# Three pairs of column groups of a projection, half of their k tiles by Strassen's scheme

## The chip, the cores and the metric

One core of a Trainium2 chip runs the whole program. The metric is the device time of one execution in microseconds (us), as the median of several runs. The core has five engines with a queue each: TensorE (PE, matrix products; PEld is its weight load), VectorE (DVE), ScalarE (ACT), GpSimd (POOL) and SyncE (SP, which here issues nearly all DMA transfers). An engine works through its queue in order.

## The reference, cut to what matters

One decoder layer for 256 tokens, D_MODEL 2048, all in f32:

```python
h = rmsnorm(x, norm_mix_g)
u = h @ w_in                     # 2048 x 12288
c_g, b_g, xa, za, q, fl, iv, og, ga, gb = split(u)      # ga, gb: 2048 columns each
ya = b_g * causal_dwconv3(c_g * xa, conv_w) * silu(za)
yb = (gated linear recurrence of q, fl, iv, normed) * silu(og)
m = sigmoid(ga) * (ya @ w_a_out) + sigmoid(gb) * (yb @ w_b_out)
x = x + m @ w_o
x = x + sigmoid(rmsnorm(x) @ w_ple_gate) * (p @ w_ple_proj)
return rmsnorm(x, final_norm_g)
```

The change touches `ga = h @ w_in[:, ...]` and `gb`, and nothing of what is computed from them.

## The kernel before, in words

Tokens lie in two tiles (t = 0, 1) of 128. A weight matrix is cut into column groups of 512 (index j) and chunks of 256 rows (index c), so a chunk of a group is two k tiles of 128 x 512, side by side in a row of 1024. One chunk is a step of the list `steps`; the list is walked in one loop over `pos`, in an order fixed by `groups`: PP (4 groups), the 24 groups of w_in with ga and gb of j last, each pair followed by A of j (w_a, 4 chunks) and B of j (w_b, 4 chunks), then O and PG. A group of w_in has 8 chunks.

Every f32 product is made of three matmuls in a rounded format (fp32r). `split` (L115) makes the high part `whi` of a chunk on ScalarE (L129) and the low part `wlo` on VectorE (L130); the activations are kept as high and low parts too (`hT` = `xh`, `xl`). `product` (L975, matmul L980) then adds high x high, high x low and low x high into a PSUM bank. So a step is 2 k tiles x 2 token tiles x 3 = 12 matmuls of 512 columns. Splits are issued three steps ahead (`LEAD`); `whi` and `wlo` have four buffers each, so a split can begin when PE has finished the step four before.

`load` (L96) fetches two chunks (1 MB) into a `raw` buffer, of which there are three, through SyncE's queue. PSUM has four banks with the tag g and four with s; a group takes two g banks.

When a group is finished its epilogue, a generator, is put on the list `active`; after every step `advance` takes each epilogue on by one `yield`. `ep_ga` and `ep_gb` turn the banks into sigmoid tiles `ga` and `gb` (ScalarE, L260). `ep_a` multiplies `ga` by A's banks (VectorE, L670), `ep_bb` `gb` by B's banks (L677); then GpSimd adds the two (L682; VectorE for j = 3), and `turned` transposes the sum: SyncE writes it to memory (`turn<-t`, L238), reads it back (`t<-turn`, L240), and VectorE turns 32 x 32 blocks (L244). ScalarE and VectorE then split it into `mh` and `ml` (L688, L689). A Tile scheduler fixes the final order in each engine's queue.

Of the kernel before, what the change touches and what calls it, by code (L numbers as in the profile page):

```python
# [23 lines left out]
CW = 512  # L24
# [11 lines left out]
_FIELD = {"c": 0, "b": 2, "xa": 4, "za": 6, "q": 8, "f": 10, "iv": 12, "og": 14, "ga": 16, "gb": 20}  # L36
IN_ORDER = [(n, j) for j in range(2) for n in ("f", "q", "iv", "og", "c", "xa", "za", "b")]
IN_ORDER += [(n, j) for j in range(4) for n in ("ga", "gb")]


PRM_GMIX, PRM_GPLE, PRM_GHG, PRM_LB, PRM_CONV = 0, 16, 32, 40, 48
# [5 lines left out]
def hybrid_kernel(ctx, tc, xT, x, pT, prm, gfin, masks, w_in, w_a, w_b, w_o, w_pg, w_pp, out):  # L47
    nc = tc.nc
# [27 lines left out]
    def nm(s):  # L76
        uid[0] += 1
        return f"{s}_{uid[0]}"

    def t4(tag="t4", bufs=None):  # L80
        bufs = bufs or {"tmp1": 8, "tmp2": 5, "tmp3": 5}[state["tmp"]]
        return pools[state["tmp"]].tile([P, 1024], F32, tag=tag, bufs=bufs, name=nm(tag))

    def bank(tag):
        return ps.tile([P, CW], F32, tag=tag, bufs=4, name=nm(tag))
# [4 lines left out]


    stream = []
    loaded = {}
    parts = {}

    def load(pos):  # L96
        w, g, c = stream[pos]
        if pos // 2 not in loaded:
            raw = wp.tile([P, 2, 2 * CW], F32, tag="raw", bufs=3, name=nm("raw"))
            loaded[pos // 2] = raw  # L100
            if FIRST <= pos < FIRST + 20:
                for i in range(2):
                    nc.sync.dma_start(out=raw[:, i, :], in_=w[g, :, c + i, :])
            elif pos >= FIRST:
                nc.sync.dma_start(out=raw, in_=w[g, :, c : c + 2, :])
        return loaded[pos // 2]

    def load_first(pos, queues):

        w, g, c = stream[pos]  # L110
        n = 2 * CW // len(queues)
        for i, eng in enumerate(queues):
            eng.dma_start(out=load(pos)[:, pos % 2, i * n : (i + 1) * n], in_=w[g, :, c, i * n : (i + 1) * n])

    def split(pos, c0=0, c1=2 * CW):  # L115
        w, g, c = stream[pos]
        src = load(pos)[:, pos % 2, :]

        pool, n = (pools["late"], 6) if (pos - state.get("late", len(steps))) % 10 < 6 and "late" in state else (wp, 4)
        if pos not in parts:  # L120
            parts[pos] = tuple(
                pool.tile([P, 2 * CW], F32R, tag=tag, bufs=n, name=nm(tag)) for tag in ("whi", "wlo")
            )
        hi, lo = parts[pos]
        s = slice(c0, c1)
        with ExitStack() as order:
            for i in state["before"].pop() if state.get("before") else ():
                order.enter_context(tc.issue_after(i))
            a = nc.scalar.activation(out=hi[:, s], in_=src[:, s], func=AF.Copy)  # L129
            v = nc.vector.tensor_tensor(  # L130
                out=lo[:, s], in0=src[:, s], in1=hi[:, s].bitcast(F32), op=ALU.subtract
            )
        state["splits"] = (a.ins, v.ins)

    groups = []
    groups += [("PP", j, w_pp, j, "pT") for j in range(4)]
    for n, (kind, j) in enumerate(IN_ORDER):
        groups.append((kind, j, w_in, n, "hT"))
        if kind == "gb":
            groups.append(("A", j, w_a, j, "yaT"))  # L140
            groups.append(("B", j, w_b, j, "ybT"))
    groups += [("O", j, w_o, j, "mT") for j in range(4)]
    groups += [("PG", j, w_pg, j, "x1T") for j in range(4)]
    steps = []
    active, done = [], 0
    for gi, (kind, j, w, g, op) in enumerate(groups):
        for c in range(w.shape[2]):
            stream.append((w, g, c))
            steps.append((gi, c))

    last_group = len(steps) - w_pg.shape[2]


    LEAD, AHEAD = 3, 4
    TOKENS, NORM = 10, 13
    FIRST = 6

# [20 lines left out]
    def gain(base, k):  # L178
        return prm_t[:, base + k : base + k + 1]
# [471 lines left out]
        nc.vector.tensor_tensor(out=lo, in0=ya, in1=hi.bitcast(F32), op=ALU.subtract)  # L651

    def ep_ga(j, psum):
        g = t4("ga", 2)
        sig(psum, g)
        state["ga", j] = g
        yield

    def ep_gb(j, psum):
        g = t4("gb", 2)  # L660
        sig(psum, g)
        state["gb", j] = g
        yield


    def ep_a(j, psum):
        g = state["ga", j]
# [285 lines left out]
    def step(e):  # L953

        with ExitStack() as order:
            for i in state["splits"] if done < len(steps) else ():
                order.enter_context(tc.issue_after(i))
            try:
                next(e)
            except StopIteration:  # L960
                active.remove(e)

    def advance():
        for e in list(active):
            step(e)
# [9 lines left out]
    def product(psum, op, k, t, hi, lo, first, last, which=(0, 1, 2)):  # L975

        oh, ol = (x[:, k, t * P : (t + 1) * P] for x in op)
        for n in which:
            a, b = ((oh, hi), (oh, lo), (ol, hi))[n]
            nc.tensor.matmul(psum, a, b, start=first and n == 0, stop=last and n == 2)  # L980

    psum = None
    for pos, (gi, c) in enumerate(steps[:last_group]):
        kind, j, w, g, opname = groups[gi]
        nch = w.shape[2]
        if kind == "PG" and j == 0 and c == 0:
            close_pool("m")
            open_pool("late", "left")
            state["late"] = done
        order = ExitStack()  # L990
        if 1 <= pos <= 4:

            order.enter_context(tc.issue_after(state["evicted"]))
        while done < min(pos + 1 + ahead(pos), len(steps)):
# [12 lines left out]
        order.close()  # L1007
        if 2 <= pos < 6:
            load_x(pos + 2)
        if pos == 4:  # L1010
            begin()
        if 0 <= pos - NORM < 4:
            add_squares(pos - NORM)
        if pos == NORM + 3:
            norm_of_x()
        if pos == NORM + 4:
            active.append(ep_f(0, waiting))
            step(active[-1])
            nc.sync.dma_start(out=mask_t, in_=masks)
        if c == 0:  # L1020
            psum = [bank("s" if kind == "PP" and j > 1 else "g") for _ in range(NT)]
        hi, lo = parts.pop(pos)
        for i in range(2):
            k = 2 * c + i
            for c0, c1 in EARLY[0][:2] if pos == 0 and i == 0 else ((0, CW),):
                s = slice(i * CW + c0, i * CW + c1)
                for n in (((0,), (2,), (1,)), ((0,), (1,), (2,)))[i] if pos == 0 else ((0, 1, 2),):
                    for t in range(NT):
                        product(
                            psum[t][:, c0:c1], state[opname], k, t, hi[:, s], lo[:, s], k == 0 and c0 == 0,  # L1030
                            k == 2 * nch - 1, n,
                        )


        if kind == "PG" and j == 0 and c < 2:
            advance()
        for q in range(done, min(done + AHEAD, len(steps)) if pos >= FIRST else 0):
            load(q)
        if 0 <= pos - TOKENS < 4:
            load_tokens(pos - TOKENS)  # L1040
        if kind != "PG" or j or c >= 2:
            advance()
        if kind == "O" and j == 0 and c == nch - 3:
            finish()
            third_part()
        if kind == "O" and j > 0 and c == 1:
            residual(j)
        if kind == "O" and j == 2 and c == 4:
            load_gfin()
        if kind == "PG" and c == 4:  # L1050
            load_projection(j)
            if j == 2:
                load_projection(3)
        if c == nch - 1:
            if kind == "f" and j == 0:

                waiting = psum
            if kind == "ga" and j == 0:
                finish()
                second_part()  # L1060
            if kind == "O" and j == 0:
# [104 lines left out]
```

## Time and profile before

| | |
|---|---|
| median of 3 runs | 824.15 us (824.03 to 824.48) |
| profiled execution, span | 822.8 us |
| mean granted clock of TensorE | 0.997 of full speed |
| PE busy, instructions | 813.9 us (99%), 4236 |
| VectorE busy | 531.4 us (65%) |
| ScalarE busy | 433.1 us (53%) |
| GpSimd busy | 91.1 us (11%) |
| DMA, mean | 228 GB/s |

The timed runs and the profiled one are different executions; the profile shows its own span, from the first to the last instruction, and no other time of it. Busy shares are means over the run, made of stages with different limits, so the prediction reads the stages that are changed. Matmuls are pipelined: a row's length (0.39 us) is longer than the distance to the next row.

### The profile page before, as it was taken

Reading aid. Unit: us, or ns where it says so; the run is one execution under the profiler, and the core shown is the slowest. Engines: PE = TensorE matmul, PEld = TensorE weight load, DVE = VectorE, ACT = ScalarE, POOL = GpSimd, SP = SyncE. Lnnn points to the kernel's source line nnn. Section 1 sums busy time; section 2 is a strip of 40 time slices with the busy share of each in tenths; the row PEclk is TensorE's granted clock in tenths of the full one; section 3 lists DMA queues with packets and bytes.
Section 4 is the critical chain, followed back from the end, with each engine's and each line's share of the span. In section 5 each row is a group of like instructions: output and inputs, shape, how many; then the busy total and the mean of one; then the engine's idle time right before and its main releaser. Section 6 shows DMA issues by size and latency. Waiting matters only on the chain.

```text
span 822.8 us, 10787 instructions
## 1 busy us (share of the span) xinstructions
PE 813.9 (99%) x4236; PEld 675.9 (82%) x4236; DVE 531.4 (65%) x620; ACT 433.1 (53%) x559; POOL 91.1 (11%) x75
## 2 busy tenths in 40 slices
PE   9999999999999999999999999999999999999996
PEld 7888888888888888888888888888888888888885
DVE  5746698967766598877646545545645656678734
ACT  7666565555564465466443543544444445566522
POOL 1000045300000064200001001000100000001210
PEclk9999999999999999999999999999999999999998
DMA  9969656648776665748555755766755698888702
GB/s 333 365 274 339 222 180 210 219 155 258 255 234 225 204 205 161 251 153 279 202 191 182 268 182 179 256 205 202 228 190 198 221 316 290 282 301 283 301 0 104
DMA packets 41524, 187.27 MB, mean 228 GB/s; under 512 B 4736, under 2 KB 14208, under 8 KB 24320
## 3 DMA queue, kind: packets, MB, share of 16 engines
q1 hardware_dynamic: 41328, 186.31, 66.0%
q8 instruction: 33, 0.54, 0.3%
q10 hardware_dynamic: 144, 0.26, 0.1%
q14 instruction: 19, 0.16, 0.0%
HBM read 172.92 MB, written 13.63 MB: 227 GB/s over the span
## 4 chain that ended last, share of the span: by engine, by line
PE 97%; DMA 1%; issue 1%; DVE 0%; ACT 0%; SPq 0%; ACTq 0%; POOLq 0%; POOL 0%
PE g L980 95%; DMA raw<-in_w_pp 1%; PE s L980 1%; PE s L394 1%; PE s L527 0%; PE s L551 0%; PE s L550 0%; PE s L549 0%; ACT xs L803 0%; DVE wlo L130 0%; ACT whi L129 0%; ACTq L1161 0%; POOLq L1161 0%; POOL tot L789 0%; ACT t L761 0%
## 5 line engine op out<-in xcount | busy, mean ns | idle before, releaser
L130 DVE TENSOR_TENSOR wlo<-raw,whi 128x1024 fp32r<-128x1024 f32 (+1 forms) x295 | 367.8, 1252 | 248.6 <-ACT whi L129 247.7
L129 ACT ACTIVATE whi<-raw 128x1024 fp32r<-128x1024 f32 (+1 forms) x295 | 307.8, 1050 | 327.1 <-PE g L980 293.7
L980 PE MATMUL g<-whi,xl 128*128 128x512 f32 (+1 forms) x912 | 351.4, 385 | 0.0
L980 PE MATMUL g<-wlo,xh 128*128 128x512 f32 (+1 forms) x912 | 351.4, 385 | 0.0
L980 PE MATMUL g<-whi,xh 128*128 128x512 f32 (+1 forms) x912 | 351.1, 386 | 0.0
L980 PEld LDWEIGHTS g<-whi,xl 128*128 128x128 f32 x912 | 171.3, 188 | 34.5
L980 PEld LDWEIGHTS g<-whi,xh 128*128 128x128 f32 x912 | 171.3, 188 | 34.2
L980 PEld LDWEIGHTS g<-wlo,xh 128*128 128x128 f32 x912 | 171.3, 188 | 34.1
L980 PE MATMUL g<-whi,mh 128*128 128x512 f32 x128 | 49.8, 389 | 0.0
L980 PE MATMUL g<-wlo,mh 128*128 128x512 f32 x128 | 49.8, 389 | 0.0
L980 PE MATMUL g<-whi,ml 128*128 128x512 f32 x128 | 49.6, 389 | 0.0
L682 POOL TENSOR_TENSOR t<-ga,gb 128x512 f32<-128x512 f32 x6 | 10.6, 1788 | 198.3 <-DVE gb L677 198.3
L980 PE MATMUL g<-whi,yaTh 128*128 128x512 f32 (+1 forms) x74 | 28.3, 389 | 0.1
L980 PE MATMUL g<-wlo,yaTh 128*128 128x512 f32 (+1 forms) x74 | 28.0, 385 | 0.2 <-DVE wlo L130 0.2
L980 PEld LDWEIGHTS g<-wlo,mh 128*128 128x128 f32 x128 | 24.0, 188 | 5.0
L980 PEld LDWEIGHTS g<-whi,mh 128*128 128x128 f32 x128 | 24.0, 188 | 5.0
L980 PEld LDWEIGHTS g<-whi,ml 128*128 128x128 f32 x128 | 24.0, 188 | 4.9
L448 POOL TENSOR_TENSOR t<-b 128x512 f32<-128x512 f32 x10 | 20.4, 2036 | 68.8 <-DMA t<-turn 41.0
L980 PE MATMUL g<-whi,yaTl 128*128 128x512 f32 (+1 forms) x74 | 27.9, 383 | 0.0
L980 PE MATMUL g<-whi,ybTh 128*128 128x512 f32 x64 | 24.9, 389 | 0.0
L980 PE MATMUL g<-wlo,ybTh 128*128 128x512 f32 x64 | 24.9, 389 | 0.0
L980 PE MATMUL g<-whi,ybTl 128*128 128x512 f32 x64 | 24.9, 389 | 0.0
(160 smaller groups left out, 518.7 us busy)
## 6 DMA issues: line engine op xcount, KB each, us to landing
raw<-in_w_in SPq DMA_DIRECT2D x85, 1024.0 KB, 5.0
raw<-in_w_o SPq DMA_DIRECT2D x16, 1024.0 KB, 6.2
raw<-in_w_pg SPq DMA_DIRECT2D x16, 1024.0 KB, 6.0
raw<-in_w_in SPq DMA_DIRECT2D x22, 512.0 KB, 8.2
turn<-t SPq DMA_DIRECT2D x72, 128.0 KB, 2.6
t<-turn SPq DMA_DIRECT2D x18, 512.0 KB, 5.4
raw<-in_w_a SPq DMA_DIRECT2D x8, 1024.0 KB, 5.2
raw<-in_w_b SPq DMA_DIRECT2D x8, 1024.0 KB, 5.2
```

Source lines behind the costliest of these rows:

```text
L129: a = nc.scalar.activation(out=hi[:, s], in_=src[:, s], func=AF.Copy)
L130: v = nc.vector.tensor_tensor(out=lo[:, s], in0=src[:, s], in1=hi[:, s].bitcast(F32), op=ALU.subtract)
L394: nc.tensor.matmul(heads(bk)[r, h, c if at is None else slice(at, at + 32)], key(h)[:, r], query(h)[:, c], start=True, stop=True, tile_pos ...
L448: nc.gpsimd.tensor_tensor(out=er, in0=br, in1=ref, op=ALU.subtract)
L682: (nc.vector if j == 3 else nc.gpsimd).tensor_tensor(out=spread(m, t), in0=blocks(ga[:, s]), in1=blocks(gb[:, s]), op=ALU.add)
L980: nc.tensor.matmul(psum, a, b, start=first and n == 0, stop=last and n == 2)
```

## The change: what it does

Groups ga and gb of j = 1, 2, 3 become one group GG of eight units (`PAIR`). Four are plain: two chunks of ga or of gb, as before (2 steps). Four are Strassen units: the same chunk of ga and gb together. With two token tiles by two k tiles on one side and two k tiles by two column groups on the other, the 2 x 2 block product is done in the form with seven products (Winograd's variant). A Strassen unit has four steps (parts) of 6, 3, 6 and 6 matmuls. Its weights are loaded in three pieces; after the split of part 0 `combine_weights` forms the sums and differences of weight blocks in place on VectorE, and part 1 uses a tile `t2` of 512 columns. The combinations of the activations are made once by `forms`, which reads xT again and runs in the steps behind ga of j = 0. Seven products per unit add up in all eight banks (four g, four s), and `ep_pair` combines the banks and takes the sigmoids.

```diff
+PAIR = ("S", 0), (0, 2), ("S", 1), (1, 2), ("S", 4), (0, 6), ("S", 5), (1, 6)
+PAIRED = [c for u, c in PAIR if u == "S"]
...
-        bufs = bufs or {"tmp1": 8, "tmp2": 5, "tmp3": 5}[state["tmp"]]
+        bufs = bufs or {"tmp1": 8, "tmp2": 4, "tmp3": 5}[state["tmp"]]
...
+            if joint[pos]:
+                nc.sync.dma_start(out=raw[:, 0, :], in_=w[g, :, c, :])
+                for i in range(2):
+                    nc.sync.dma_start(
+                        out=raw[:, 1, i * CW : (i + 1) * CW], in_=w[g + 1, :, c, (1 - i) * CW : (2 - i) * CW]
+                    )
...
+        if joint[pos]:
+            src = load(pos)[:, part == 3, :]
+            if part == 1:
+                src, c1 = half[unit_of[pos]], CW
...
+    def combine_weights(pos):
+        b = load(pos).rearrange("p i (k c) -> p (i k) c", k=2)
+        t2 = half[unit_of[pos]] = pools["tmp2"].tile([P, CW], F32, tag="t2", bufs=2, name=nm("t2"))
+        nc.vector.tensor_tensor(
+            out=b[:, 0:4:3, :], in0=b[:, 0:3:2, :], in1=b[:, 3:4, :].to_broadcast([P, 2, CW]), op=ALU.subtract
+        )
+        nc.vector.tensor_tensor(out=t2, in0=b[:, 2, :], in1=b[:, 0, :], op=ALU.add)
+        nc.vector.tensor_tensor(out=b[:, 1, :], in0=b[:, 1, :], in1=t2, op=ALU.subtract)
...
     def ep_ga(j, psum):
-        g = t4("ga", 2)
+        g = t4("ga", 1)
...
+    def forms():
+        for n in range(0, len(PAIRED), 2):
+            raw, f = t4(), t4()
...
+                nc.sync.dma_start(out=r[:, u], in_=xT[:, 2 * c : 2 * c + 2, :])
...
+            nc.vector.scalar_tensor_tensor(out=s1, in0=a21, scalar=-1.0, in1=a22, op0=ALU.mult, op1=ALU.subtract)
+            nc.vector.scalar_tensor_tensor(out=s2, in0=s1, scalar=-1.0, in1=a11, op0=ALU.mult, op1=ALU.subtract)
+            yield
+            nc.vector.tensor_tensor(out=s3, in0=a11, in1=a21, op=ALU.subtract)
+            nc.vector.tensor_tensor(out=s4, in0=a12, in1=s2, op=ALU.subtract)
...
+    def ep_pair(j, e, m):
+        ga, gb = t4("ga", 1), t4("gb", 1)
...
+        nc.scalar.activation(out=gb[:, a], in_=m[1], func=AF.Copy)
+        add(ga[:, a], gb[:, a], e[0, 0])
+        add(gb[:, a], gb[:, a], m[6])
+        yield
+        add(gb[:, b], gb[:, a], m[7])
+        add(ga[:, b], gb[:, b], e[1, 0])
+        yield
...
+        add(pair, pair, m[5].rearrange("p (o c) -> p o c", o=1).to_broadcast([P, 2, CW]))
...
+            add(gb[:, s], gb[:, s], e[t, 1])
...
+        elif part == 0:
+            add(1, *tile_of(2 * c, 0), a)
+            add((0, 0), *tile_of(2 * c + 1, 0), b)
+        elif part == 1:
+            add(6, *state["S", c, 1], a)
+        elif part == 2:
+            add(5, *state["S", c, 0], a)
+            add((1, 0), *tile_of(2 * c + 1, 1), b)
+        else:
+            add((0, 1), *state["S", c, 3], a)
+            add(7, *state["S", c, 2], b)
```

In `pair_products` every `add` is three matmuls of 512 columns, as in `product`.

More of the change, by code (lines that the diff above doesn't have):

```diff
@@ L92, in hybrid_kernel @@
     stream = []
+    unit_of, part_of, joint = [], [], []
     loaded = {}
     parts = {}
+    half = {}
     def load(pos):
         w, g, c = stream[pos]
-        if pos // 2 not in loaded:
+        if unit_of[pos] not in loaded:
             raw = wp.tile([P, 2, 2 * CW], F32, tag="raw", bufs=3, name=nm("raw"))
-            loaded[pos // 2] = raw
-            if FIRST <= pos < FIRST + 20:
+            loaded[unit_of[pos]] = raw
+            if joint[pos]:
[4 more added lines that the diff above has]
+                    )
+            elif FIRST <= pos < FIRST + 20:
                 for i in range(2):
@@ L105, in load @@
                 nc.sync.dma_start(out=raw, in_=w[g, :, c : c + 2, :])
-        return loaded[pos // 2]
+        return loaded[unit_of[pos]]
     def load_first(pos, queues):
@@ L112, in load_first @@
         for i, eng in enumerate(queues):
-            eng.dma_start(out=load(pos)[:, pos % 2, i * n : (i + 1) * n], in_=w[g, :, c, i * n : (i + 1) * n])
+            eng.dma_start(
+                out=load(pos)[:, part_of[pos], i * n : (i + 1) * n], in_=w[g, :, c, i * n : (i + 1) * n]
+            )
     def split(pos, c0=0, c1=2 * CW):
-        w, g, c = stream[pos]
-        src = load(pos)[:, pos % 2, :]
+        part = part_of[pos]
+        src = load(pos)[:, part % 2, :]
+        if joint[pos]:
+            src = load(pos)[:, part == 3, :]
+            if part == 1:
+                src, c1 = half[unit_of[pos]], CW
         pool, n = (pools["late"], 6) if (pos - state.get("late", len(steps))) % 10 < 6 and "late" in state else (wp, 4)
@@ L133, in split @@
         state["splits"] = (a.ins, v.ins)
+        if joint[pos] and part == 0:
+            combine_weights(pos)
+    def combine_weights(pos):
[3 more added lines that the diff above has]
+            out=b[:, 0:4:3, :], in0=b[:, 0:3:2, :], in1=b[:, 3:4, :].to_broadcast([P, 2, CW]), op=ALU.subtract
+        )
+        nc.vector.tensor_tensor(out=t2, in0=b[:, 2, :], in1=b[:, 0, :], op=ALU.add)
+        nc.vector.tensor_tensor(out=b[:, 1, :], in0=b[:, 1, :], in1=t2, op=ALU.subtract)
     groups = []
@@ L137, in hybrid_kernel @@
     for n, (kind, j) in enumerate(IN_ORDER):
-        groups.append((kind, j, w_in, n, "hT"))
+        if j == 0 or kind not in ("ga", "gb"):
+            groups.append((kind, j, w_in, n, "hT"))
+        elif kind == "ga":
+            groups.append(("GG", j, w_in, n, "hT"))
         if kind == "gb":
@@ L145, in hybrid_kernel, with add_step @@
     active, done = [], 0
-    for gi, (kind, j, w, g, op) in enumerate(groups):
-        for c in range(w.shape[2]):
-            stream.append((w, g, c))
-            steps.append((gi, c))
+    def add_step(gi, c, w, g, k, part, s):
+        stream.append((w, g, k))
+        steps.append((gi, c))
+        unit_of.append((unit_of[-1] if unit_of else -1) + (part == 0))
+        part_of.append(part)
+        joint.append(s)
+    for gi, (kind, j, w, g, op) in enumerate(groups):
+        if kind != "GG":
+            for c in range(w.shape[2]):
+                add_step(gi, c, w, g, c, len(steps) % 2, False)
+            continue
+        for n, (u, c) in enumerate(PAIR):
+            for part in range(4 if u == "S" else 2):
+                add_step(gi, (n, part), w, g if u == "S" else g + u, c if u == "S" else c + part, part, u == "S")
     last_group = len(steps) - w_pg.shape[2]
-    LEAD, AHEAD = 3, 4
+    LEAD = 3
     TOKENS, NORM = 10, 13
@@ L659, in ep_gb @@
     def ep_gb(j, psum):
-        g = t4("gb", 2)
+        g = t4("gb", 1)
         sig(psum, g)
@@ L663, in ep_gb @@
         yield
+    def forms():
+        for n in range(0, len(PAIRED), 2):
+            raw, f = t4(), t4()
+            r = raw.rearrange("p (u k t) -> p u k t", u=2, k=2)
+            for u in range(2):
+                c = PAIRED[n + u]
+                nc.sync.dma_start(out=r[:, u], in_=xT[:, 2 * c : 2 * c + 2, :])
+            for u in range(2):
+                yield
+                for k in range(2):
+                    h = r[:, u, k, :]
+                    nc.scalar.activation(
+                        out=h, in_=h, func=AF.Identity, scale=gain(PRM_GMIX, 2 * PAIRED[n + u] + k)
+                    )
+            yield
+            a11, a12, a21, a22 = (r[:, :, k, t * P : (t + 1) * P] for t in range(2) for k in range(2))
+            s1, s2, s3, s4 = (f[:, i * 2 * P : (i + 1) * 2 * P].rearrange("p (u t) -> p u t", u=2) for i in range(4))
+            nc.vector.scalar_tensor_tensor(out=s1, in0=a21, scalar=-1.0, in1=a22, op0=ALU.mult, op1=ALU.subtract)
[3 more added lines that the diff above has]
+            nc.vector.tensor_tensor(out=s4, in0=a12, in1=s2, op=ALU.subtract)
+            yield
+            hi, lo = (pools["tmp2"].tile([P, 1024], F32R, tag="S" + x, bufs=2, name=nm("S" + x)) for x in "hl")
+            nc.scalar.activation(out=hi, in_=f, func=AF.Copy)
+            nc.vector.tensor_tensor(out=lo, in0=f, in1=hi.bitcast(F32), op=ALU.subtract)
+            for u in range(2):
+                for i in range(4):
+                    s = slice((2 * i + u) * P, (2 * i + u + 1) * P)
+                    state["S", PAIRED[n + u], i] = hi[:, s], lo[:, s]
+            yield
@@ new lines, in ep_pair, with add @@
+    def ep_pair(j, e, m):
+        ga, gb = t4("ga", 1), t4("gb", 1)
+        state["ga", j], state["gb", j] = ga, gb
+        a, b = slice(0, CW), slice(CW, 2 * CW)
+        def add(out, x, y):
+            nc.vector.tensor_tensor(out=out, in0=x, in1=y, op=ALU.add)
+        nc.scalar.activation(out=gb[:, a], in_=m[1], func=AF.Copy)
+        add(ga[:, a], gb[:, a], e[0, 0])
+        add(gb[:, a], gb[:, a], m[6])
+        yield
+        add(gb[:, b], gb[:, a], m[7])
+        add(ga[:, b], gb[:, b], e[1, 0])
+        yield
+        pair = gb.rearrange("p (t c) -> p t c", t=2)
+        add(pair, pair, m[5].rearrange("p (o c) -> p o c", o=1).to_broadcast([P, 2, CW]))
+        for t in range(NT):
+            s = slice(t * CW, (t + 1) * CW)
+            nc.scalar.activation(
+                out=ga[:, s], in_=ga[:, s], func=AF.Sigmoid, scale=state["rstd1"][:, t : t + 1]
+            )
+        yield
+        for t in range(NT):
+            s = slice(t * CW, (t + 1) * CW)
+            add(gb[:, s], gb[:, s], e[t, 1])
+        yield
+        for t in range(NT):
+            s = slice(t * CW, (t + 1) * CW)
+            nc.scalar.activation(
+                out=gb[:, s], in_=gb[:, s], func=AF.Sigmoid, scale=state["rstd1"][:, t : t + 1]
+            )
@@ L980, in product, with ask_ahead, pair_products, add @@
             nc.tensor.matmul(psum, a, b, start=first and n == 0, stop=last and n == 2)
+    def ask_ahead():
+        q = done
+        if q < len(steps):
+            for u in range(unit_of[q], unit_of[q] + 2 + (part_of[q] > 0)):
+                if u in first_of:
+                    load(first_of[u])
+    def pair_products(at):
+        n, part = at
+        u, c = PAIR[n]
+        hi, lo = parts.pop(pos)
+        a, b = slice(0, CW), slice(CW, 2 * CW)
+        def add(name, xh, xl, s):
+            k = left[name]
+            for i, (x, y) in enumerate(((xh, hi), (xh, lo), (xl, hi))):
+                nc.tensor.matmul(
+                    banks[name], x, y[:, s], start=k == total[name] and i == 0, stop=k == 1 and i == 2
+                )
+            left[name] -= 1
+        def tile_of(k, t):
+            return (x[:, k, t * P : (t + 1) * P] for x in state["hT"])
+        if u != "S":
+            for i in range(2):
+                for t in range(NT):
+                    add((t, u), *tile_of(2 * c + 2 * part + i, t), (a, b)[i])
+        elif part == 0:
[9 more added lines that the diff above has]
+            add(7, *state["S", c, 2], b)
+    first_of = {}
+    for q, u in enumerate(unit_of):
+        first_of.setdefault(u, q)
+    plain = [4 * sum(u == i for u, _ in PAIR) for i in range(2)]
+    total = {(t, g): plain[g] + len(PAIRED) * ((t, g) != (1, 1)) for g in range(2) for t in range(NT)}
+    total.update({n: len(PAIRED) for n in (1, 5, 6, 7)})
     psum = None
@@ L1019, in hybrid_kernel @@
             nc.sync.dma_start(out=mask_t, in_=masks)
+        if kind == "GG":
+            if c == (0, 0):
+                left = dict(total)
+                banks = {n: bank("g" if type(n) is tuple else "s") for n in total}
+            pair_products(c)
+            ask_ahead()
+            if not joint[pos] or c[1] % 2:
+                advance()
+            if c == (max(n for n, (u, _) in enumerate(PAIR) if u == "S"), 3):
+                m = {n: banks[n] for n in (1, 5, 6, 7)}
+                active.append(ep_pair(j, banks, m))
+                step(active[-1])
+            continue
         if c == 0:
@@ L1036, in hybrid_kernel @@
             advance()
-        for q in range(done, min(done + AHEAD, len(steps)) if pos >= FIRST else 0):
-            load(q)
+        if pos >= FIRST:
+            ask_ahead()
         if 0 <= pos - TOKENS < 4:
@@ L1060, in hybrid_kernel @@
                 second_part()
+                active.append(forms())
+                step(active[-1])
             if kind == "O" and j == 0:
```

## The prediction

> **What bounds the kernel now.** I read the page's head first, then the chain of waits, then the stages that the change touches.
>
> ```profile
> span 822.8 us, 10787 instructions
> ...
> PE 813.9 (99%) x4236; PEld 675.9 (82%) x4236; DVE 531.4 (65%) x620; ACT 433.1 (53%) x559; POOL 91.1 (11%) x75
> ...
> PEclk9999999999999999999999999999999999999998
> ...
> PE 97%; DMA 1%; issue 1%; DVE 0%; ACT 0%; SPq 0%; ACTq 0%; POOLq 0%; POOL 0%
> ```
>
> TensorE (PE) works without a break at its granted clock, and 97% of the chain that ended last is PE. So a matmul taken away shortens the run, as long as nothing else becomes late in the same stage. The stages in question, first ga and gb of j = 1, then A and B of j = 1 (windows; span, PE, PE weight load, VectorE, ScalarE, GpSimd):
>
> ```profile
> 444.25:487.80 43.55, 43.55 (x194) 36.06 (x193) 23.38 (x20) 19.81 (x20) 3.54 (x2) 1.00 0.64 217
> 487.80:509.60 21.80, 21.80 (x98) 18.06 (x97) 11.27 (x11) 9.24 (x10) 0.00 (x0) 1.00 0.58 195
> ```
>
> VectorE (DVE) has 20 us idle in the first and 10 in the second. The change spends just this idle time. The pace of PE stands in its timeline (start, length):
>
> ```profile
> 439.72 0.39 PE L980 MATMUL g<-wlo,ybTh 128*128 128x512 f32 x1
> ...
> 444.25 0.39 PE L980 MATMUL g<-whi,xh 128*128 128x512 f32 x1
> ...
> 449.92 0.39 PE L980 MATMUL g<-wlo,xh 128*128 128x512 f32 x1
> ```
>
> 46 rows from first to last, so 10.20 us / 45 = 0.2267 us a matmul. Pair j = 1 begins at 444.25, my zero below.
>
> **What it removes.** A chunk of 256 k rows of ga and gb is 8 block products of 3 matmuls, by Strassen 7. Four chunks in each of three pairs: 12 products, 36 matmuls, 36 x 0.2267 = 8.16 us. The instruction order of the changed kernel has 36 PE rows fewer. If nothing else happened: 824.15 - 8.16 = 815.99.
>
> **What it adds on VectorE and ScalarE.**
>
> ```profile
> L130 DVE TENSOR_TENSOR wlo<-raw,whi 128x1024 fp32r<-128x1024 f32 x290 | 365.0, 1263 | 247.2 <-ACT whi L129 246.3
> L130 DVE TENSOR_TENSOR wlo<-raw,whi 128x512 fp32r<-128x512 f32 x3 | 2.0, 688 | 1.3 <-ACT whi L129 1.3
> L455 DVE TENSOR_TENSOR y<-b,tot 128x1024 f32<-128x1024 f32 x2 | 2.4, 1217 | 0.0
> L129 ACT ACTIVATE whi<-raw 128x1024 fp32r<-128x1024 f32 x290 | 305.4, 1059 | 323.3 <-PE g L980 293.7 <-issue 10.0 <-DMA raw<-in_w_pg 8.2
> ```
>
> A Strassen unit needs three splits of 1024 columns and one of 512 where two of 1024 stood, and combine_weights: one 1024-wide subtraction with a broadcast (nearest row: 1.22) and two of 512 (0.69). In the timeline of VectorE, at the start of the pair, an operation alone takes 1.23, and one that stands ready behind another begins 1.14 after it:
>
> ```profile
> 443.97 1.28 DVE L677 TENSOR_TENSOR gb<-gb,g 128x512 f32<-128x512 f32 x2
> 445.55 1.62 DVE L130 TENSOR_TENSOR wlo<-raw,whi 128x1024 fp32r<-128x1024 f32 x1 [0.31 <-ACT whi L129]
> ...
> 450.99 1.23 DVE L130 TENSOR_TENSOR wlo<-raw,whi 128x1024 fp32r<-128x1024 f32 x1 [1.49 <-ACT whi L129]
> ...
> 457.86 1.25 DVE L244 STREAM_TRANSPOSE t<-t 128x1024 f32<-128x1024 f32 x1 [0.20 <-DMA t<-turn]
> 459.15 1.22 DVE L130 TENSOR_TENSOR wlo<-raw,whi 128x1024 fp32r<-128x1024 f32 x1
> 460.29 1.22 DVE L689 TENSOR_TENSOR ml<-t,mh 128x1024 fp32r<-128x1024 f32 x1
> ```
>
> A Strassen unit and the plain unit behind it are thus six 1024-wide and three 512-wide operations: between 6 x 1.14 + 3 x 0.69 = 8.9 and 6 x 1.23 + 3 x 0.69 = 9.4 us, against 45 matmuls or 10.20 us of PE. VectorE goes from half idle to about 90% busy, before the epilogues: of the group before, 1.28 + 1.25 + 1.22 fall into the pair, and of the pair's own seven additions (six 512-wide, one 1024-wide, 5.4) some two thirds into A. ScalarE has 5.5 x 1.06 = 5.8 of 10.20: not the bound. So what counts is where VectorE's queue is late, and by how much.
>
> **Where it is late.** Behind a pair's start stands the epilogue of the B group before: GpSimd (POOL) adds, SyncE sends the sum out and back (`turned`), and SyncE's queue is in order, so a weight load behind it waits. Rows of the timelines of GpSimd, SyncE and ScalarE, of the tile `ga` (least, median, longest ns), and of the DMA issues by stretch (size, us to landing; the 6.3 is the load of 450.24, the 4.9 the way back of 452.88, the 6.9 the load of 453.31):
>
> ```profile
> 444.79 3.54 POOL L682 TENSOR_TENSOR t<-ga,gb 128x512 f32<-128x512 f32 x2 [74.84 <-DVE gb L677]
> L682 POOL TENSOR_TENSOR t<-ga,gb x6: 1294/1788/2282, 444.8 to 576.5; 128x512 f32<-128x512 f32 x6
> 448.36 1.78 SPq L238 DMA_DIRECT2D turn<-t  x4
> 450.24 0.40 SPq L105 DMA_DIRECT2D raw<-in_w_in  x1
> 452.88 0.34 SPq L240 DMA_DIRECT2D t<-turn  x1
> 453.31 10.20 SPq L105 DMA_DIRECT2D raw<-in_w_in  x3
> raw<-in_w_in SPq DMA_DIRECT2D x1, 1024.0 KB, 6.3
> t<-turn SPq DMA_DIRECT2D x1, 512.0 KB, 4.9
> raw<-in_w_in SPq DMA_DIRECT2D x1, 1024.0 KB, 6.9
> 449.89 1.06 ACT L129 ACTIVATE whi<-raw 128x1024 fp32r<-128x1024 f32 x1 [1.66 <-PE g L980]
> ```
>
> The load of 450.24 lands at 456.54, which is 8.21 after POOL's end at 448.33. In the old kernel it is wanted long after. In the new order of SyncE that place holds the second plain unit (P'), wanted at 14.96: units are 21, 24, 21 matmuls, 66 x 0.2267.
>
> When does it land? The POOL operation that ran beside VectorE took 2.28, the other 1.29. In the new kernel VectorE works through both: ScalarE has the last part of the first Strassen unit ready at 1.26 (1.06 from 0.20 behind B's last step, as its row at 449.89 begins 0.20 behind the 24th matmul), and three splits, slowed as the one of 1.62 is, end at 2.9, 4.5 and 5.9 (wanted at 3.6, 5.0 and 7.7, so PE does not notice). So I take 2.28 twice: POOL ends at 0.54 + 4.56 = 5.10, the load lands at 13.31. From there a rigid chain runs in the new order of VectorE: split of P' (hand-off 0.04 between engines, as from ScalarE's end at 450.95 to VectorE's start at 450.99; 1.06; 0.04; 1.23) done at 15.68; five ready operations at 1.14 (the transpose, a split of P', the first split of the third Strassen unit, the `ml` split, the 1024-wide combination) to 21.38; two dependent combinations at 0.69 to 22.76; ScalarE 0.04 + 1.06; VectorE 0.04 + 1.23: 25.13. That is part 2 of the third Strassen unit. PE gets there after 99 matmuls, 22.44, and wants the low half in its second matmul, 22.67. **PE waits 2.46 us in each pair.** The waits on P' (0.5) and part 1 of that unit are inside this sum.
>
> The transpose in it is not late itself: the way back lands 9.45 after POOL's end as now, at 14.55. Nor is the third unit's own load, next in SyncE's queue: 4.98 after POOL's end it is issued, the two further pieces 0.8 later, and 6.9 on all has landed, at 17.8; the combination wants it at 20.2, and the first half, which the first split wants at 16.8, comes as the first piece.
>
> Other places, by the same queue: the second Strassen unit starts on VectorE at 5.8; first split 7.05, combinations 8.2, 8.9 and 9.6, part 1 at 10.2, part 2 (ScalarE in between) 12.0, part 3 13.1; wanted at 11.8, 12.5 and 13.8. The fourth unit profits from the wait. At the end A's second bank wants the fourth addition when it is just ready: cost 0, at the worst 0.3, unless VectorE is slower. `forms` brings twice four 256-wide and one 1024-wide operation on VectorE, eight and two on ScalarE; nearest rows:
>
> ```profile
> L203 DVE SCALAR_TENSOR_TENSOR xl<-t,prm_t,xh 128x256 fp32r<-128x256 f32 x32 | 13.8, 479 | 0.6
> L202 ACT ACTIVATE xh<-t,prm_t 128x256 fp32r<-128x256 f32 x32 | 14.0, 509 | 1.5 <-DVE t L244 1.5
> ```
>
> That is 6.3 and 6.2 us, and 1 MB of DMA. It runs in gb, A and B of j = 0, where VectorE waits 1.49 for each split as above, and three splits are made ahead: hidden; if not, 1 us. The pieces of a Strassen load take two more issues of some 0.4 each, before their data are wanted: hidden. The single copies of `ga`, `gb` and the t4 buffers come free in the A and B before.
>
> Sum: 824.15 - 8.16 + 3 x 2.46 = 823.4. Of the profiled execution only the span is shown, 822.8, which is 1.35 below the median of the three timed runs; I leave those 1.35 as they are, so the new span would be 822.0.
>
> **Rivals.**
>
> Faster: the load lands as now. If POOL still ends at 4.08, the chain moves up by 1.02, the waits are 1.44 each: 824.15 - 8.16 + 4.3 = 820.3. For it: VectorE has small gaps. Against: it has hardly any between 1.3 and 5.6. Chance 0.22.
>
> Faster, by a lock: GpSimd and VectorE could exclude one another instead of slowing one another. POOL's two operations of 1.29 would have one split between them and end at 0.54 + 1.29 + 1.23 + 1.29 = 4.35, and the load would no longer be last. VectorE's queue from 4.35 then gives P' at 15.03 (1.23, 3 x 1.14, 2 x 0.69 to 10.38; ScalarE and VectorE 2.37; 2 x 1.14), 0.65 before 15.68: waits of 1.81, 821.4. The row speaks against it: both were slowed at once, 1.62 for 1.23 and 2.28 for 1.29, though POOL began first. Chance 0.08. The Trainium skill has this rule (SBUF — State Buffer, "Who interferes with whom": the shared port pair is an exclusive lock, and a VectorE operation with two SBUF inputs falls under it against GpSimd's reads); the trace here does not agree with it.
>
> Slower: VectorE does not overlap its operations when its queue is full, and each takes its full 1.23. Then 5 x 0.09 makes the wait 2.91, and the 18 operations between there and the addition that A's second bank waits for come 18 x 0.09 = 1.6 later, of which 0.45 are in the longer wait: 1.15 at A. 824.15 - 8.16 + 3 x 4.06 = 828.2. It turns to slower at 0.05 an operation. For it: most of the new operations wait for one before. Against: 459.15 to 460.29. Chance 0.22.
>
> It doesn't do what it says, VectorE never being late (816.0) or `forms` holding up the splits behind it on ScalarE: 0.04.
>
> **The numbers.** Forecast case 0.44: waits of 2.0 to 3.2 a pair, 822.0 to 825.6, likeliest 823.4. A difference of 0.2% (1.65 us: 822.5 and 825.8) is about what a measurement of this kernel can tell. Faster: 0.22 + 0.08 + 0.04 of the forecast case + 0.02 = 0.36. Same: 0.38 of the forecast case. Slower: 0.22 + 0.02 + 0.02 = 0.26. Range from the early load to the full queue: 820.0 to 828.2.
>
> **What would show it.** PE rows 36 fewer at 0.2267; in each pair one gap cluster of some 2.5 us, from the second plain unit (about 15 us in) to part 2 of the third Strassen unit (about 22 to 25), released by `wlo`, none elsewhere; POOL's addition 4.4 to 4.6 long; the load behind `turn` landing at 13 to 13.6. Wrong: waits in every Strassen unit, or at A, or a clock below 1.00 in these stages.

## The result, and the profile after

The changed kernel takes 821.96 us (median of 17 runs, 820.77 to 823.49), the kernel before 824.2 us on the same chips (17 runs). The ratio is 0.997, 95% interval 0.9963 to 0.9977: 2.2 us faster by the medians, where 0.8 was forecast and 8.2 would have been the whole saving. The profiled execution of the changed kernel took 820.92 us, its span is 819.1; so it is one of the quicker ones.

The page of the changed kernel (span; busy time; clock; the chain that ended last, by engine and by line):

```profile
span 819.1 us, 10931 instructions
...
PE 808.1 (99%) x4199; PEld 668.1 (82%) x4200; DVE 604.2 (74%) x711; ACT 456.0 (56%) x596; POOL 91.2 (11%) x75
...
PEclk9999999999999999999999999999999999999998
...
PE 89%; DVE 4%; issue 3%; ACT 2%; DMA 1%; ACTq 0%; POOLq 0%; POOL 0%; DVEq 0%
```

VectorE has grown from 531 to 604 us, and 8% of the chain has left PE: there are now places where PE waits. The windows of pair j = 1 and of A and B of j = 1 (columns as in the prediction) say where:

```profile
443.45:485.77 42.32, 41.73 (x181) 33.43 (x180) 40.02 (x40) 24.68 (x27) 3.54 (x2) 1.00 0.65 223
485.77:507.58 21.81, 21.81 (x97) 17.94 (x96) 16.93 (x19) 10.27 (x12) 0.00 (x0) 1.00 0.56 194
```

VectorE is busy for 40.0 of 42.3 us in the pair, and A and B are as quick as before. The rows of PE at which pairs begin (`L1114`) and end (`L1094` with `yaTh`) give the length of each pair:

```profile
443.45 0.39 PE L1114 MATMUL s<-whi,xh 128*128 128x512 f32 x1
...
485.77 0.39 PE L1094 MATMUL g<-whi,yaTh 128*128 128x512 f32 x1
...
507.58 0.39 PE L1114 MATMUL s<-whi,xh 128*128 128x512 f32 x1
...
549.81 0.39 PE L1094 MATMUL g<-whi,yaTh 128*128 128x512 f32 x1
...
571.57 0.39 PE L1114 MATMUL s<-whi,xh 128*128 128x512 f32 x1
...
614.37 0.39 PE L1094 MATMUL g<-whi,yaTh 128*128 128x512 f32 x1
```

42.32, 42.23 and 42.80 us. 180 matmuls at 0.2267 are 40.81, so PE waits 1.51, 1.42 and 1.99 us: 4.9 in all, forecast 7.4. All waits of pair 1 are in two places, about 448.5 and 466 to 468; the chain of waits, at its start and in the third Strassen unit (start, length):

```profile
446.42 0.72 DVE wlo L150
447.13 1.02 issue
...
459.52 1.25 DVE wlo L150 x2
460.78 0.96 issue
461.74 1.22 DVE ml L803
462.96 1.15 DVE raw L161
464.13 0.70 DVE t L164
...
464.94 0.64 ACT whi L149
465.61 0.70 DVE wlo L150
466.35 0.28 issue
466.63 1.05 ACT whi L149
467.68 0.04 issue
467.73 0.50 PE g L1114
```

From 459.5 to the dependent combinations, VectorE's queue is that of the forecast, operation by operation: splits, `ml`, the wide combination, the first dependent one (464.13), the second. Two things are different. One is what lies in front of it, as the experiments show. The other is the last link. The waits of PE, at the first plain unit and in the third Strassen unit (PE's timeline):

```profile
448.79 0.50 PE L1114 MATMUL g<-wlo,xh 128*128 128x512 f32 x1 [0.19 <-DVE wlo L150]
...
466.35 0.50 PE L1114 MATMUL s<-wlo,Sh 128*128 128x512 f32 x1 [0.22 <-DVE wlo L150]
...
467.73 0.50 PE L1114 MATMUL g<-whi,Sh 128*128 128x512 f32 x1 [0.17 <-ACT whi L149]
468.06 0.39 PE L1114 MATMUL s<-whi,Sh 128*128 128x512 f32 x1
468.30 0.39 PE L1114 MATMUL s<-wlo,Sh 128*128 128x512 f32 x1
```

The forecast had PE wait for the low half of part 2. That low half is read at 468.30 and costs nothing, because PE's queue has two high-half products of part 3 in front of it (467.73 and 468.06). PE waits instead for the low half of part 1 (466.35) and for part 3's high half from ScalarE (467.73), some 0.5 us each.

### The profile page after: what moved, and what is told of

It is laid out like the page before. It is cut to its first block, busy times and chain, and to the rows that moved or that the text cites. A ratio compares the mean times of both kernels' runs of the same rounds, so it can differ in the third digit from the quotient of the medians.

```text
span 819.1 us, 10931 instructions
## 1 busy us (share of the span) xinstructions
PE 808.1 (99%) x4199; PEld 668.1 (82%) x4200; DVE 604.2 (74%) x711; ACT 456.0 (56%) x596; POOL 91.2 (11%) x75
## 4 chain that ended last, share of the span: by engine, by line
PE 89%; DVE 4%; issue 3%; ACT 2%; DMA 1%; ACTq 0%; POOLq 0%; POOL 0%; DVEq 0%
PE g L1094 80%; PE g L1114 5%; DVE wlo L150 3%; ACT whi L149 2%; PE s L1114 1%; DMA raw<-in_w_in 1%; DVE raw L161 1%; PE s L1094 1%; PE s L440 1%; PE s L972 0%; DVE ml L803 0%; DVE t L164 0%; PE s L573 0%; PE s L596 0%; PE s L597 0%
## 5 line engine op out<-in xcount | busy, mean ns | idle before, releaser
L150 DVE TENSOR_TENSOR wlo<-raw,whi 128x1024 fp32r<-128x1024 f32 (+1 forms) x307 | 382.5, 1262 | 172.4 <-ACT whi L149 171.2
L1094 PE MATMUL g<-whi,xl 128*128 128x512 f32 (+1 forms) x720 | 276.7, 384 | 0.0
L1094 PE MATMUL g<-wlo,xh 128*128 128x512 f32 (+1 forms) x720 | 276.7, 384 | 0.0
L1094 PE MATMUL g<-whi,xh 128*128 128x512 f32 (+1 forms) x720 | 276.4, 385 | 0.0
L1094 PEld LDWEIGHTS g<-whi,xl 128*128 128x128 f32 x720 | 135.3, 188 | 27.0
L1094 PEld LDWEIGHTS g<-whi,xh 128*128 128x128 f32 x720 | 135.3, 188 | 27.0
L1094 PEld LDWEIGHTS g<-wlo,xh 128*128 128x128 f32 x720 | 135.3, 188 | 26.5
L1094 PE MATMUL g<-whi,mh 128*128 128x512 f32 x128 | 49.8, 389 | 0.0
L1094 PE MATMUL g<-wlo,mh 128*128 128x512 f32 x128 | 49.8, 389 | 0.0
L1094 PE MATMUL g<-whi,ml 128*128 128x512 f32 x128 | 49.6, 389 | 0.0
L1114 PE MATMUL g<-wlo,xh 128*128 128x512 f32 x120 | 47.1, 392 | 0.4 <-DVE wlo L150 0.2
L1114 PE MATMUL g<-whi,xl 128*128 128x512 f32 x120 | 46.8, 390 | 0.0
L1114 PE MATMUL g<-whi,xh 128*128 128x512 f32 x120 | 46.7, 389 | 0.0
L1094 PEld LDWEIGHTS g<-whi,ml 128*128 128x128 f32 x128 | 24.0, 188 | 5.0
L1094 PEld LDWEIGHTS g<-wlo,mh 128*128 128x128 f32 x128 | 24.0, 188 | 5.0
L1094 PEld LDWEIGHTS g<-whi,mh 128*128 128x128 f32 x128 | 24.0, 188 | 4.9
L1094 PE MATMUL g<-whi,yaTl 128*128 128x512 f32 (+1 forms) x74 | 27.9, 384 | 0.0
L1094 PE MATMUL g<-wlo,yaTh 128*128 128x512 f32 (+1 forms) x74 | 27.9, 383 | 0.0
```

The source lines that it names most:

```text
L150: v = nc.vector.tensor_tensor(out=lo[:, s], in0=src[:, s], in1=hi[:, s].bitcast(F32), op=ALU.subtract)
L1114: nc.tensor.matmul(banks[name], x, y[:, s], start=k == total[name] and i == 0, stop=k == 1 and i == 2)
```

## Experiments

The table gives, for each kernel, the waits of PE in the three pairs (length of the pair, read as above, less its matmuls at 0.2267) and in A behind them, and the time that the waits alone would give: the kernel before on the same chip (823.96 for the first four, 824.02 for the others), less the matmuls left out, plus the waits.

| kernel | waits in pairs | in A | by the waits | measured | ratio, 95% interval |
|---|---|---|---|---|---|
| e4 changed kernel again | 1.80, 1.44, 2.72 | 0, 0, 0.06 | 821.8 | 821.57 | 0.997 (0.996 to 0.9981) |
| e1 transpose put off | 0.68, 0.42, 0.82 | 0 | 817.7 | 818.07 | 0.9929 (0.9916 to 0.9941) |
| e2 no combinations | 0.37, 0.38, 0.38 | 0.09, 0.11, 0.09 | 817.2 | 817.61 | 0.9922 (0.991 to 0.9935) |
| e3 two units a pair | 0.34, 0.51, 0.40 | 0.50, 0.13, 0.49 | 822.3 | 822.69 | 0.9986 (0.9977 to 0.9995) |
| e5 addition on VectorE | 0.81, 0.79, 0.77 | 0 | 818.2 | 818.72 | 0.9932 (0.992 to 0.9945) |
| e6 both | 0.02, 0.01, 0 | 0 | 815.9 | 816.41 | 0.9904 (0.9889 to 0.9919) |
| e7 one combination more | 3.71, 3.47, 3.58 | 0 | 826.6 | 826.61 | 1.0029 (1.0018 to 1.004) |
| e8 transpose put off, load ahead | 0.51, 0.38, 0.38 | 0.13, 0.14, 0.14 | 817.5 | 818.21 | 0.9931 (0.9918 to 0.9944) |

The waits account for every kernel to 0.7 us or better. Most measured times lie about half a microsecond above. In the profiles 0.2 to 0.3 of it lies behind the last matmul of the run: from its start to the end of the span 8.1 us before, 8.3 to 8.4 in the nine later profiles. Why, and where the rest is, stays open.

**e1.** `turned(m, 2 if j == 3 else 3)` with 18 in place of the 3.

```diff
-        m = yield from turned(m, 2 if j == 3 else 3)
+        m = yield from turned(m, 2 if j == 3 else 18)
```

> For j < 3 the transpose of the merged sum and its split (ml) are put off by 15 more steps, from the middle of the next pair into its A group; the write-out, the load behind it and the read-back stay where they are. Theory Q (VectorE's queue is late by itself: transpose and ml split, 2.3 us, stand in front of the third Strassen unit): the waits of 1.4 to 2.0 us a pair go, 816.0 to 817.0 us. Theory L (the weight load behind turn lands late and starts the chain): the second plain unit still waits for it where it lands after 12.9, up to 0.5 us a pair: 816.5 to 817.5. Rival R (the waits come from somewhere else in the pair, or the late transpose stops A): 820 or more.

818.07 us, 3.5 faster than the changed kernel on the same chip, and above both ranges, 1.1 over Q's upper end and 0.6 over L's. The waits in the third unit are gone, as Q says. What stays is a wait of 0.4 us at the first plain unit in each pair, which neither theory had, and, in the first and the third pair, one of 0.2 and 0.4 at the second plain unit. There the load lands 13.3 and 13.4 after the pair's start; in the second pair, which has no such wait, 12.4.

**e2.** `combine_weights(pos)` replaced by handing part 1 the raw weights.

```diff
-            combine_weights(pos)
+            half[unit_of[pos]] = load(pos)[:, 1, :CW]
```

> Leaves out combine_weights, that is three VectorE operations (2.6 us) in each Strassen unit; part 1 is split from the raw weights instead, so ga and gb are not the reference's. PE's work is the same. Theory Q: VectorE needs some 6.4 us less in front of the third unit's part 2, no wait is left, 816.0 us (815.8 to 816.6). Theory L: the load's landing is unchanged, the third unit's chain is 2.6 shorter, so a wait of 0 to 0.5 a pair at the second plain unit stays: 816.0 to 817.5. If the saving of 36 matmuls were not 8.16 us, the time shows it here.

817.61 us, 1.0 over Q's range and 0.1 over L's: again without any wait in the third unit, and again with 0.37 us at the first plain unit. PE's pace holds, so the 36 matmuls are worth 8.16 us. The pairs' first waits do not come from the combinations.

**e3.** The unit list with two Strassen units.

```diff
-PAIR = ("S", 0), (0, 2), ("S", 1), (1, 2), ("S", 4), (0, 6), ("S", 5), (1, 6)
+PAIR = ("S", 0), (0, 2), (1, 2), (0, 4), (1, 4), (0, 6), ("S", 1), (1, 6)
```

> Two Strassen units a pair instead of four (the first unit and the last but one), the rest plain, same paired order and epilogue. PE has 18 matmuls fewer than the kernel before instead of 36: 4.08 us. VectorE has plain units between and is not late. Both theories: 824.2 - 4.1 = 820.1 us (819.8 to 820.6). If pairing the groups or the epilogue of the pair cost something by themselves, it is slower than that by just this cost.

822.69 us, 2.6 slower than expected: a miss. Half of it is the same first wait; the other half is at A, where the weight load of PE waits for an addition of the pair's epilogue that reads the bank which A needs. The waits of pair 1 and A behind it (who waited for whom, us in all, times, longest):

```profile
PEld g L1094 <- DVE ga L753: 0.6, 1, 0.6
PEld g L1114 <- DVE wlo L150: 0.5, 1, 0.5
```

The prediction had called this place "just ready". The addition in e3, then the matmul that waits for it, then the same addition in the changed kernel:

```profile
486.52 0.68 DVE L753 TENSOR_TENSOR ga<-gb,g 128x512 f32<-128x512 f32 x1
...
487.25 0.50 PE L1094 MATMUL g<-whi,yaTh 128*128 128x512 f32 x1 [0.19 <-DVE ga L753]
...
486.55 0.68 DVE L753 TENSOR_TENSOR ga<-gb,g 128x512 f32<-128x512 f32 x1
```

VectorE is not later here. In e3 the addition ends at 487.20, 1.21 after A's start (485.99); in the changed kernel at 487.23, 1.46 after it (485.77), and there A waits 0.06 at most. The order of PE's queue differs. In e3 the fifth matmul of A waits for the bank, wanted 0.91 after A's start; in the changed kernel the first seven run while the addition is still at work, and the eighth, 1.59 in, finds it done. So the price of this place hangs on the order that the scheduler chose.

**e4.** The changed kernel again.

> The changed kernel unchanged, on the same chip as the three others, for comparison: 821 to 823 us; its pairs wait 1.4 to 2.0 us each in the profile.

821.57 us. This profile has other waits than the first one, 1.80, 1.44 and 2.72, and with them one sees what sets them. The load behind `turn` is issued at 449.75, 514.02 and 578.02 and lands 6.7, 5.7 and 7.7 later; in the first profile of the changed kernel at 449.55, 513.59 and 577.58, landing 5.6, 6.3 and 7.0 later. The issue and the landing of the earliest and the latest in e4 (pair 2, which begins at 508.01, and pair 3, at 572.02):

```profile
514.02 0.39 SPq L118 DMA_DIRECT2D raw<-in_w_in  x1
raw<-in_w_in SPq DMA_DIRECT2D x1, 1024.0 KB, 5.7
...
578.02 0.38 SPq L118 DMA_DIRECT2D raw<-in_w_in  x1
raw<-in_w_in SPq DMA_DIRECT2D x1, 1024.0 KB, 7.7
```

All six, from SyncE's timeline and the DMA issues of both profiles (landing less the pair's start):

| load lands at | 11.70 | 11.71 | 12.31 | 12.81 | 13.01 | 13.70 |
|---|---|---|---|---|---|---|
| PE waits in the pair | 1.51 | 1.44 | 1.42 | 1.80 | 1.99 | 2.72 |

Above some 12.4 the wait is the landing less 11.0, three times over; below it stays at 1.4 to 1.5, and something else sets it. (The prediction's chain says landing less 10.85.) This fits the scatter of the changed kernel's time over 2.7 us: the two profiled executions, with waits of 4.9 and 6.0 in all, took 820.92 and 822.16. No other execution of it has a profile.

**e5.** The additions of `ga` and `gb` on VectorE.

```diff
-            (nc.vector if j == 3 else nc.gpsimd).tensor_tensor(
+            nc.vector.tensor_tensor(
```

> The two additions of L682 (two SBUF inputs) go from GpSimd to VectorE for j < 3 too; all else as in the changed kernel. Theory K (lock: beside a GpSimd addition a split does not run at all; GpSimd's two additions cost VectorE 1.5 us in the pair's first two splits): VectorE pays 1.2 and gets 1.5 back, the wait of 0.4 at the first plain unit goes, the load behind turn lands 2 us earlier and is never late; about 1.1 us of wait a pair are left at the third unit: 819.1 us (818.5 to 820). Theory S (as predicted: both engines slowed by a third): VectorE pays 1.2 and gets 0.8 back, 1.9 a pair: 821.5 or more.

818.72 us: K, not S. One takes work off GpSimd, gives it to the engine that is late, and the kernel is 2.9 us faster than the changed one, each against the kernel before on its own chip. Not all of it is the lock: the load behind `turn` lands earlier too, 10.5 to 11.1 after the pair's start. But even against the pairs of the changed kernel whose load is early (1.42 to 1.51) the wait is 0.6 to 0.7 shorter. The timelines at the pair's start show why. The changed kernel's VectorE (start, length):

```profile
443.21 1.28 DVE L791 TENSOR_TENSOR gb<-gb,g 128x512 f32<-128x512 f32 x2
444.79 6.21 DVE L150 TENSOR_TENSOR wlo<-raw,whi 128x1024 fp32r<-128x1024 f32 x4 [0.31 <-ACT whi L149]
```

Its GpSimd:

```profile
444.11 3.54 POOL L796 TENSOR_TENSOR t<-ga,gb 128x512 f32<-128x512 f32 x2 [74.96 <-DVE gb L791]
```

GpSimd's two additions, and the first two of these splits, by tile (least, median, longest ns; first and last start):

```profile
L796 POOL TENSOR_TENSOR t<-ga,gb x2: 1294/1785/2276, 444.1 to 445.4; 128x512 f32<-128x512 f32 x2
L150 DVE TENSOR_TENSOR wlo<-raw,whi x2: 1699/2010/2320, 444.8 to 446.4; 128x1024 fp32r<-128x1024 f32 x2
```

e5, VectorE:

```profile
443.54 1.28 DVE L791 TENSOR_TENSOR gb<-gb,g 128x512 f32<-128x512 f32 x2
444.74 1.29 DVE L796 TENSOR_TENSOR t<-ga,gb 128x512 f32<-128x512 f32 x2
445.94 4.63 DVE L150 TENSOR_TENSOR wlo<-raw,whi 128x1024 fp32r<-128x1024 f32 x4
```

Four splits take 4.63 us alone and 6.21 beside the additions. They take turns: GpSimd adds from 444.11 to 445.40; the split that came at 444.79 ends 1.70 later, at 446.49, a full split after 445.40 but for the overlap; GpSimd's second addition starts at 445.40, waits for that split and ends at 447.65, 2.28 long; the split that came at 446.36 waits for it and ends at 448.68. If the two slowed each other, the first addition would be longer the earlier a split comes beside it; e7 shows that it is not. That last split was wanted at 448.44 (443.45 + 4.99); in PE's timeline the matmul that reads it starts at 448.79, and the next one is 0.1 late as well. That is the wait of some 0.4 at the first plain unit (0.9 in e7), in every kernel that has the additions on GpSimd, and in neither e5 nor e6.

**e6.** e1 and e5 together.

> Both changes: additions on VectorE, and transpose and ml split put off by 15 steps into A. Theory Q with K: nothing is late any more in the pairs, 824.0 - 8.16 = 815.8 us (815.6 to 816.6). If a wait at the first plain unit of 0.4 a pair stays, K is wrong: 817.0 or more.

816.41 us, 0.9904 of the kernel before: 7.6 us faster than it and the best of all. Its first pair (window as above):

```profile
444.07:484.90 40.83, 40.83 (x181) 33.79 (x180) 38.34 (x40) 24.58 (x26) 0.00 (x0) 1.00 0.69 237
```

Its chain by engine:

```profile
PE 98%; issue 1%; DMA 1%; DVE 0%; ACT 0%; ACTq 0%; POOLq 0%; POOL 0%
```

The pair lasts as long as its matmuls, 40.83 us, with VectorE 94% busy; in the whole run VectorE is as busy as in the changed kernel (604.5 and 604.2 us). The cost of Strassen here is not VectorE's total, but what stands in its queue in front of the third unit.

**e7.** One dependent 512-column operation more in each unit.

```diff
+        nc.vector.tensor_tensor(out=t2, in0=b[:, 2, :], in1=b[:, 0, :], op=ALU.add)
```

> One combination of 512 columns (t2) is made twice in each Strassen unit: one dependent VectorE operation of 0.73 us more a unit. Two units of a pair lie in front of the third unit's part 2. Theory Q (VectorE's queue is late from the pair's start on): 1.46 us more a pair, 821.6 + 4.4 = 826.0 us. Theory L (the chain starts when the late load lands): 0.73 more a pair, 823.8 us. In pairs whose load lands before 12.4 after the start Q holds, in the others something between.

826.61 us: 5.0 more than e4, and 0.6 over Q's 826.0. Pair 2 is the one that separates the theories. Its load lands 12.7 after the start, so L, with landing less 11.0 and one operation of 0.73, gives 2.4; it waits 3.47, 2.0 more than the pairs of the changed kernel with an early load. In pairs 1 and 3 the load lands at 13.85 and 13.72, and L gives 3.58 and 3.45 where 3.71 and 3.58 were measured, so they do not tell. The 2.0 are more than two operations (1.46): the first unit's, made in B, counts in part as well. In pair 1 the four splits at the start are

```profile
444.74 6.60 DVE L150 TENSOR_TENSOR wlo<-raw,whi 128x1024 fp32r<-128x1024 f32 x4
```

and end 8.00 after the pair's start (443.34), in the changed kernel 7.55 after it. So VectorE's queue is late from before the pair's start: Q, and somewhat more strongly than it was put.

GpSimd's two additions and the first two of these splits, by tile, bear on e5's reading:

```profile
L797 POOL TENSOR_TENSOR t<-ga,gb x2: 1302/1794/2287, 444.4 to 445.7; 128x512 f32<-128x512 f32 x2
L150 DVE TENSOR_TENSOR wlo<-raw,whi x2: 2086/2202/2317, 444.7 to 446.7; 128x1024 fp32r<-128x1024 f32 x2
```

Here the first split comes 0.30 after the first addition's start (444.44), in the changed kernel 0.68. The addition takes 1.30 and 1.29; the split 2.09 and 1.70, so that it ends 2.39 and 2.38 after the addition's start. The earlier it comes, the longer it waits, and the addition does not notice: the two exclude one another, and do not slow one another.

**e8.** As e1, and two steps of pause before the write-out; the load of the second plain unit then stands behind the first of four write-outs.

```diff
+        for _ in range(0 if j == 3 else 2):
+            yield
-        m = yield from turned(m, 2 if j == 3 else 3)
+        m = yield from turned(m, 2 if j == 3 else 16)
```

> The additions stay on GpSimd; transpose and ml split are put off into A, and the weight load of the second plain unit is issued behind the first of the four write-outs instead of the fourth. The late landing goes (0.3 of the waits of 0.7, 0.4 and 0.8 that are left with the transpose put off); the wait of 0.4 at the first plain unit stays: 817.2 us (816.8 to 817.8). If that wait goes too, it came from the load and not from GpSimd: 816.0.

818.21 us, above the expected range, and not faster than e1 (818.07). The pairs did what was expected, 0.4 to 0.5 each at the first plain unit and no wait for the load, which lands 10.9 to 11.4 after the start; but 0.13 to 0.14 in each A (as in e3, PE's queue has the high-half product that wants the late bank as the fifth matmul), and the remainder that most kernels have, take the gain back. As a comparison with e1 it is inconclusive; that the first wait does not come from the load it does show.

## Why the prediction was right, and where its steps were not

- **The saving.** 36 matmuls at 0.2267, 8.16 us: right. e6, in which nothing waits, has pairs of 40.82 us.
- **The bound.** That VectorE's queue would be late in the third Strassen unit of each pair and nowhere in the second and fourth: right, and VectorE's queue there runs in the predicted order with the predicted lengths. The last link was wrong: PE waits for part 1's low half and part 3's high half, not for part 2's low half, as its queue is in another order. A wait at the first plain unit, 0.4, was not forecast at all. 1.14 from start to start holds for a full queue: five operations took 5.77 us, so 4 x 1.14 + 1.22. The slower rival, an engine that does not overlap, fell.
- **What starts the chain.** Wrong in size: the term "POOL ends at 5.10, the load lands at 13.31". GpSimd's additions took 3.54 us as before and ended at 4.20; the load landed at 11.7 to 13.7, in the mean 12.5. So the wait was 1.42 to 2.72 and not 2.46 throughout, and where the load is early the queue by itself leaves 1.4 to 1.5. The rival with the early load had priced this at 1.44, but by another step: in it the load still starts the chain. That the queue itself sets the wait was the lock rival's step, priced at 1.81.
- **The lock.** I gave the exclusion of GpSimd and VectorE a chance of 0.08 and read the row against it: one addition 2.28, the other 1.29, one split 1.62, "both slowed at once". The row gives a least and a longest time and not which came first. It was the first addition that took 1.29, held VectorE off, and the second that waited for a split. The rows of before read the same way: the first addition ends at 446.09, the split at 447.17, 2.38 after that addition's start, and the second addition at 448.33. The Trainium skill states such a lock (SBUF — State Buffer, "Who interferes with whom": GpSimd and VectorE share one port pair, only one of them has it at a time, and a VectorE operation needs it against GpSimd's reads when both its inputs are in SBUF, not when one is). By e5, e7 and the timelines the trace agrees: 1.6 us lost over two splits, and nothing by the operations with one input in PSUM (`L791`, 1.28 in both kernels, though GpSimd's first addition ran beside them for only 0.4 us). Its price in the rival, 821.4, came near 821.96; the wait that it makes at the first plain unit I had not followed, as the forecast lets that split end at 4.5 instead of 5.2.
- **What should cost nothing.** `forms` did: pair 1 starts at 443.45, before the change at 444.25, so not later. The A bank: 0.06 at most in the changed kernel, 0.5 in e3, so "just ready" was right and is fragile.
- **The forecast** of 823.4 was 1.4 us high, and it came that near because errors cancelled. GpSimd's end was put 0.90 too late in each pair; with that alone mended the waits are 1.56 and the time 820.7, which is too low. The six measured pairs waited 1.81 in the mean, as the queue has its own floor and some loads land late, and about half a microsecond is in no wait at all. Of the six waits only one (2.72) lay in the 2.0 to 3.2 of the forecast case, and 821.96 is just below the lower end of its times, 822.0. So the mechanism, a late queue of VectorE, was right; the closeness of the number was partly luck.

## What to carry to other kernels

When a change spends an engine's idle time, do not compare totals: lay out that engine's queue from the step where the work arrives, and ask which operation that nobody is waiting for stands in front of the one that PE waits for. Here a transpose and a split for a product that begins 50 to 180 us later took 2.3 us of VectorE's queue in each pair, and moving them away saved 3.5 us in all; with two additions a pair moved as well, a gain of 2.4 us became 7.6.

In a group of rows, least and longest say nothing about order; with two engines in it, ask which came first before reading a slowdown.

## What the runs showed of the hardware that I had not expected

A GpSimd addition and a VectorE split with two inputs in SBUF run in turn, not side by side: 1.29 and 1.23 us of work for which the profile shows up to 2.28 and 2.32, the waiting counted as busy. The engine that was busy for 11% of the run held up the one that was 95% busy in the pair.

The same 1 MB load, at the same place of the same queue, lands 5.6 to 7.7 us after its issue (six pairs in two profiles). Where a chain begins with it, the wait follows it, and the kernel's time seems to: 820.8 to 823.5 over 17 runs, against 816.3 to 816.8 over 4 of e6, where it lands 10.1 to 10.2 after the pair's start and nothing waits for it.
